# Weight sums in DRAM paced by ScalarE, in 4096 byte packets and for one product more, and the order of reads, heads and rows around them

## The chip, the cores and the metric

The kernel runs on one core of a Trainium2 chip. The metric is the device time of one execution in microseconds (us); the median of several runs is compared. A core has TensorE (PE, with PEld for its weight loads), VectorE (DVE), ScalarE (ACT), GpSimd (POOL) and SyncE (SP). Here SP issues most loads from DRAM, and POOL issues stores and all DMAs that add to what is already there (accumulate). Every engine, and each of these two issue queues, works through its instructions in the order in which the program wrote them, and waits on semaphores.

## What is computed

Two layers over 512 positions of width 2048. In each layer one projection of x feeds three groups of heads, every head's output is gated, one output projection follows, then a residual and a layer norm:

```python
h = jnp.einsum('bsd,dn->bsn', x, w_in)
(fq, fk, fv, fg, f_logit, dq, dk, dv, dg, iq, ik, iw, mq, mg) = jnp.split(h, offsets, axis=-1)
y_fox = fox_attention(heads(fq, 6), heads(fk, 6), heads(fv, 6), cum_logf) * silu(fg)
y_dsa = dsa_attention(rope(heads(dq, 6)), rope(heads(dk, 6)), heads(dv, 6), q_idx, k_idx, w_idx) * silu(dg)
y_mem = memory_attention(heads(mq, 4), k_mem, v_mem) * silu(mg)
y = jnp.einsum('bsn,nd->bsd', jnp.concatenate([y_fox, y_dsa, y_mem], -1), w_out)
x = layer_norm(ALPHA * x + y, ln_gain, ln_bias)
```

`fox_attention` (6 "f" heads) is causal attention with a bias per position; `dsa_attention` (6 "d" heads) attends to the 128 keys that an indexer picks for each query; `memory_attention` (4 "m" heads) attends to 256 memory tokens. All in float32; the kernel writes each float32 operand as a high and a low float32r part and takes three matmuls per product.

## The kernel before

**Stages of a layer.** Memory keys and values ("kv"); the indexer's projection ("index"); the value stage ("values"), which projects most columns; the head stage ("heads"), in which the last projections and the attention of the heads are interleaved; the output projection ("out"); and the layer norm, which makes the next layer's x.

**Chunks and halves.** All weights lie in DRAM as chunks of [128, 2048] (1 MB), in the order of use. A chunk is loaded in two halves of [128, 1024] into a pool of seven `raw` buffers (`load_w`, line 351), two chunks ahead where a buffer is free. `split_w` (line 433) turns a half into `whi` on ScalarE and `wlo` = raw - whi on VectorE, three halves ahead of the matmuls that use it. A chunk of a value or output product takes 24 matmuls of 128x512, 12 for each half.

**Seven products instead of eight.** The value and output projections use a Strassen-like scheme (`PRODUCTS`, line 82): P1, P7, Q4, P2, Q6, Q5, Q3, each with a left operand (A11, S3, A22, A12, S2, S1, S4) and a right operand that is a block of the weights or a sum of blocks (T1 to T4). The seven run over pairs of column blocks (six pairs for the values, two for the output). In the value stage P1, P7, P2, Q6, Q4 run, pair by pair; in the head stage Q5 and Q3. A product's two row blocks (`st` = 0, 1) accumulate in two PSUM banks. P2 goes on in the banks of P1, Q6 and Q4 in those of P7; Q3 goes on in the banks of Q5 right behind it.

**How the sums of weights are made.**
- "sum": in DRAM, by two DMAs on POOL's queue for a key of 1 MB: a copy of the first block (`sums[key]` made in `weight_sums`, line 565), later an accumulate of the second (`add_weights`, line 562). Before, these are T1 of all six value pairs, T3 of the first value pair, T3 of both output pairs: 18 keys a layer.
- "pair": T3 of the other value pairs. The second block is loaded into `other` slots, and VectorE adds it (`pair_w`, line 398).
- "grown": Q6's and Q4's weights grow out of those of P7, by VectorE in the value stage (`make_w`), by accumulating DMAs on POOL in the output stage (`grow_w`).
- "both": T1 of the output, S1's weights in Q5: quarters are loaded into slots by SP (`load_both`, 12 halves ahead) and the second block is added to them by accumulating DMAs on POOL (`add_both`, 8 halves ahead).

**What sets the order.** `all_sums` is a generator that issues one sum DMA and then lets some ticks pass (`paced`); in the value stage a chunk is one tick and a sum comes every two ticks, in "kv" and "heads" none. Outside the value stage `pool_waits` (line 551) goes ahead of each sum: VectorE writes a one-column `mark`, and a POOL instruction reads it into `seen`, so that POOL comes to the DMA no earlier than VectorE comes to the mark. In the value stage there is no mark. `val_out` (line 1255) reads both finished banks of a product when its last chunk is over. In the head stage a planner with a model clock (`flow`, `advance`) puts steps of the heads between the matmuls of the chunks: among the steps that fit, the one of the flow with the lowest age. At most `ACTIVE` heads are under way, and each start also needs `enough` slots, of 69 in all. `out_operands` prepares the output's left operands as such a flow. `top_keys` picks the indexer's keys on VectorE during the value stage; `residual_rows` (line 1480), in layer 1, loads 12 tiles of the layer's input on SP, multiplies and adds gain and bias on VectorE, and stores them on POOL, one tile per three ticks.

```python
        paced: yield {"out": 3, "index": 1 + n % 2}.get(now[1], steps)     # steps = PACE = 2
        enough: return live() + n <= (OUT_LIVE if now[1] == "out" else SLOTS - KT - 11)     # 44, or 42
        fits: return f[0] <= max(t, clock.at[eng]) and clock.at[eng] <= t + (SOON if now[1] == "heads" else LATER)
```

Of the kernel before, what the change touches and what calls it, by code (L numbers as in the profile page):

```python
# [20 lines left out]
DM = 2048  # L21
# [16 lines left out]
SLOTS = 69  # L38
# [20 lines left out]
BOTH_LOAD, BOTH_ADD = 12, 8  # L59
EARLY_AT = {0: 1, 1: 1, 2: 1, 3: 1, 4: 2, 5: 2}  # L60
ACTIVE = 2
OUT_LIVE = 44
# [44 lines left out]
PAIRED = {"T1": ((0, 0), (0, 1)), "T3": ((0, 1), (1, 1))}  # L107
# [26 lines left out]
def stream():  # L134
# [5 lines left out]
    def product(kind, l, name, pair, gs=(0, 1)):  # L140
        right = PRODUCTS[name][2]
        for g in gs:
            at = lambda step: where[kind, l, 2 * pair + step[1], 2 * step[0] + g]
            if name in GROWN:
                of, step = GROWN[name]
                src = ("grown", (of, at(step)))
            elif kind == "val" and right == "T3" and pair >= IN_DRAM:
                src = ("pair", tuple(at(step) for step in PAIRED[right]))
            elif kind == "out" and right == "T1":
                src = ("both", tuple(at(step) for step in PAIRED[right]))  # L150
            elif isinstance(right, str):
                src = ("sum", (kind, l, right, pair, g))
            else:
                src = ("wall", at(right))
# [103 lines left out]
def kernel(  # L258
# [42 lines left out]
    def enough(n):  # L301
        return live() + n <= (OUT_LIVE if now[1] == "out" else SLOTS - KT - 11)
# [48 lines left out]
    def load_w(i, pieces=2, some=(0, 1)):  # L351
        if i < len(chunks) and chunks[i][4][0] not in ("grown", "both"):
# [25 lines left out]

    def load_both(n):

        i, h = divmod(n, 2)
        if i < len(chunks) and chunks[i][4][0] == "both":
            src = half(wall[chunks[i][4][1][0]], h)
            t = raw.setdefault(i, [None, None])
            t[h] = [slot("both") for _ in range(2)]
            for c in range(2):
                nc.sync.dma_start(t[h][c], src[:, c * 512:(c + 1) * 512])

    def add_both(n):

        i, h = divmod(n, 2)
        if i < len(chunks) and chunks[i][4][0] == "both":
            src = half(wall[chunks[i][4][1][1]], h)
            for c in range(2):
                nc.gpsimd.dma_start(raw[i][h][c], src[:, c * 512:(c + 1) * 512], accum_op=ALU.add)

# [154 lines left out]
    def pool_waits():  # L551

        mark, seen = small("mark", 1), small("seen", 1)
        nc.vector.tensor_copy(mark, mhalf)
# [7 lines left out]
    def add_weights(key, src):  # L562
        nc.gpsimd.dma_start(sums[key], src, accum_op=ALU.add, max_dma_last_dim=4 * DM)

    def weight_sums(kind, l, names, pairs, some=(0, 1)):

        for name in names:
            for n in some:
                step = SUM_STEPS[name][n]
                for pair in pairs:  # L570
                    for g in range(2):
                        key = (kind, l, name, pair, g)
                        src = block(kind, l, pair, g, step)
                        if now[1] != "values":
                            pool_waits()
                        if n:
                            add_weights(key, src)
                        else:
                            sums[key] = dram.tile([P, DM], F32, name=uid("sum"))
                            nc.gpsimd.dma_start(sums[key], src)  # L580
# [19 lines left out]
    def all_sums():  # L600


        for l in range(DEPTH):
            yield from paced(value_sums(l))
            yield from paced(weight_sums("out", l, ("T3",), range(2)))
# [649 lines left out]
    def val_out(name, pair, ps):  # L1255


        if pair == PAIRS - 1:
            val_done.append(name)
            for k in [k for k in vleft if k[0] == PRODUCTS[name][1]]:  # L1260
                del vleft[k]
        j = 2 * pair
        for st in range(2):
            m1, m7 = ("M1", pair, st), ("M7", pair, st)
            if name == "P2" and j in VALUES:
                d = slot("vraw")
                nc.scalar.activation(d, ps[st], AF.Copy)
                begin(store_v(d, (j, st)), 1)
            elif name in ("P1", "P7"):
                d = vraw[m1 if name == "P1" else m7] = slot("vraw")  # L1270
                nc.scalar.activation(d, ps[st], AF.Copy)
            elif name == "P2":
                begin(store_turned(halves(ps[st]), (j, st)), 1)
            elif name == "Q6":
                d, e = slot("vraw"), vraw.pop(m7)
                nc.vector.scalar_tensor_tensor(d, ps[st], -1.0, vraw[m1], op0=ALU.mult,
                                               op1=ALU.subtract)
                nc.vector.tensor_tensor(e, e, d, op=ALU.add)
                begin(store_v(d, (j + 1, 2 + st)), 1)
                begin(store_v(e, (j + 1, st)), 1)  # L1280
            elif name == "Q4":
                d = vraw.pop(m1)
                nc.vector.tensor_tensor(d, d, ps[st], op=ALU.add)
                begin((store_v if j in VALUES else store_sum)(d, (j, 2 + st)), 1)
            elif j + 1 in VALUES:
                d = slot("vraw")
                nc.scalar.activation(d, ps[st], AF.Copy)
                begin(store_v(d, (j + 1, st + 2 * (name == "Q5")), True), 1)
            else:
                d = vraw.pop(("base", st))  # L1290
                nc.vector.tensor_tensor(d, d, ps[st], op=ALU.add)
                begin(store_sum(d, (j + 1, st + 2 * (name == "Q5"))))

    def load_base(name, pair):

        for st in range(2):
            r = st + 2 * (name == "Q5")
            assert stored[2 * pair + 1, r] == 1
            t = vraw["base", st] = slot("vraw")
# [277 lines left out]
    for i, (kind, l, j, col, _) in enumerate(chunks):  # L1577
# [17 lines left out]
        elif kind == "vs":  # L1595
# [3 lines left out]
            if col == 0:  # L1599
                if opens:  # L1600
                    chains[VAL_CHAIN[name], pair] = [bank("v"), bank("v")]
                if name in ("Q5", "Q3") and 2 * pair + 1 not in VALUES:
                    load_base(name, pair)
# [6 lines left out]
        for h in range(2):  # L1610
            n = 2 * i + h
            grow_w(n + 2)
            add_both(n + BOTH_ADD)
            load_both(n + BOTH_LOAD)
# [50 lines left out]
            elif kind == "vs":  # L1665
                for st in range(2):
                    for e in range(2):
# [3 lines left out]
                        advance()  # L1671
            elif kind == "mv":
# [40 lines left out]
        elif kind == "vs":  # L1713
            if col == 1:
                val_out(name, pair, zs)
# [43 lines left out]
        if kind == "vs" and (name, pair, col) == ("Q6", 0, 1) and l > 0:  # L1759
            begin(residual_rows(l), whole=True)  # L1760
        if kind == "vs" and (name, pair, col) == ("Q4", PAIRS - 1, 1):
            start_heads(l)
        if kind == "vs" and (name, pair, col) == ("Q5", PAIRS - 1, 0):
            flow(out_operands())
# [102 lines left out]
```

## Time and profile before

| | us |
|---|---|
| median of three runs | 1975.38 |
| lowest and highest | 1970.56, 1983.48 |
| the profiled execution, its own time | 1974.53 |
| its span, first to last instruction | 1972.8 |

The granted TensorE clock of the profiled execution is 0.983 on average. Nearly every instruction has line 242, that of the helper that records it, so the profile is read by the names of tiles: `v` are the banks of the value products, `c` those of other projections, `z` the output's, `vxh`/`vxl` and `xh`/`xl` the left operands' parts, `yh`/`yl` those of the output, `vraw` what is read from the banks. A row of a group reads: line, engine, operation, out<-in, shapes, xcount | busy us, mean ns | idle time of the engine just before these instructions, and what ended it. A row of the timeline: start, duration, engine, line, operation, tiles, and in brackets the idle time before. Of the DMA queues, q1 is SP's and q0 is POOL's.

The stages by the trace: layer 0's values about 148 to 569 us, heads to 791, output and norm to 985; layer 1's values 1129 to 1549, heads to 1771, output to 1962. Instructions that issue DMAs and those that wait are not counted as busy.

### The profile page before, as it was taken

To read this page: it belongs to the slowest core of one execution; us is meant where nothing else is said; L and a number is where in the kernel's file an instruction comes from. 1 tells how busy PE (TensorE), PEld (TensorE's weight loads), DVE (VectorE), ACT (ScalarE), POOL (GpSimd) and SP (SyncE) were. 2 spreads that over 40 slices of the span, in tenths; PEclk is the share of its full clock that TensorE was granted. 3 is DMA by queue.
4 is the path that set the end of the run, shared out by engine and by line. 5 is a ranking of instruction groups with operands and counts; after the bars stand their busy time and mean duration, and the time that the engine had idled before them with its cause. 6 is when DMAs were issued, how large, how long until landed. Compare 5 with 4: busy or idle time off the path is not lost.

```text
span 1972.8 us, 26387 instructions
## 1 busy us (share of the span) xinstructions
PE 1876.5 (95%) x8930; PEld 1576.4 (80%) x8930; DVE 1612.7 (82%) x2581; ACT 1081.5 (55%) x1702; POOL 384.4 (19%) x561
## 2 busy tenths in 40 slices
PE   9999799899999999999999998999999989999997
PEld 8998688687888787776899987877788878878865
DVE  6889588688788888787896897898887888888778
ACT  5775244344357777564576753343354577776443
POOL 0121011010133111252021111111110332112522
PEclk9999899899999999999999999999999999999999
DMA  9876878885589899999687878988955898999996
GB/s 350 302 218 203 275 239 248 260 240 199 171 224 255 256 238 247 206 258 242 203 296 251 221 213 271 302 264 283 285 202 150 240 258 241 249 226 239 275 250 149
DMA packets 233508, 478.38 MB, mean 242 GB/s; under 512 B 94289, under 2 KB 110673, under 8 KB 227933
## 3 DMA queue, kind: packets, MB, share of 16 engines
q1 hardware_dynamic: 190716, 306.78, 49.9%
q0 software_dynamic: 42080, 168.87, 33.5%
q8 instruction: 70, 1.15, 0.2%
q10 hardware_dynamic: 576, 1.05, 0.1%
q14 instruction: 66, 0.53, 0.1%
HBM read 400.05 MB, written 135.29 MB: 271 GB/s over the span
## 4 chain that ended last, share of the span: by engine, by line
PE 54%; DMA 19%; DVE 15%; ACT 5%; issue 5%; SPq 0%; POOL 0%; DVEq 0%; ACTq 0%; POOLq 0%
PE v L242 25%; PE c L242 16%; DMA other<-in_wall_dram 8%; PE z L242 7%; DVE wlo L242 6%; DMA both<-in_wall_dram 4%; DMA raw<-in_wall_dram 3%; PE po L242 2%; DVE raw L242 2%; ACT whi L242 2%; DVE acc L242 1%; PE ix L242 1%; DMA grown<-in_wall_dram 1%; PE s L242 1%; DVE z L242 1%
## 5 line engine op out<-in xcount | busy, mean ns | idle before, releaser
L242 ACT ACTIVATE whi<-raw 128x1024 fp32r<-128x1024 f32 (+1 forms) x481 | 502.4, 1055 | 527.6 <-PE v L242 238.1
L242 DVE TENSOR_TENSOR wlo<-raw,whi 128x1024 fp32r<-128x1024 f32 (+1 forms) x481 | 581.2, 1217 | 105.0 <-ACT whi L242 103.9
L242 PE MATMUL v<-wlo,vxh 128*128 128x512 f32 x768 | 304.2, 396 | 28.0 <-DVE wlo L242 27.7
L242 PE MATMUL v<-whi,vxh 128*128 128x512 f32 x768 | 305.9, 398 | 18.1 <-DVE vraw L242 13.0
L242 PE MATMUL v<-whi,vxl 128*128 128x512 f32 x768 | 302.1, 393 | 0.0
L242 PE MATMUL v<-wlo,xh 128*128 128x512 f32 x576 | 226.3, 393 | 11.6 <-DVE wlo L242 11.6
L242 PE MATMUL v<-whi,xh 128*128 128x512 f32 x576 | 225.4, 391 | 4.7 <-ACT whi L242 4.7
L242 PE MATMUL v<-whi,xl 128*128 128x512 f32 x576 | 225.1, 391 | 0.0
L242 PE MATMUL c<-xh,whi 128*128 128x512 f32 (+1 forms) x544 | 197.9, 364 | 0.0
L242 PE MATMUL c<-xh,wlo 128*128 128x512 f32 (+1 forms) x544 | 197.8, 364 | 0.0
L242 PE MATMUL c<-xl,whi 128*128 128x512 f32 (+1 forms) x544 | 197.7, 363 | 0.0
L242 PEld LDWEIGHTS v<-wlo,vxh 128*128 128x128 f32 x768 | 145.9, 190 | 63.8 <-DVE wlo L242 35.9
L242 PEld LDWEIGHTS v<-whi,vxh 128*128 128x128 f32 x768 | 145.8, 190 | 51.6 <-issue 9.8
L242 PE MATMUL z<-whi,yh 128*128 128x512 f32 (+1 forms) x434 | 173.1, 399 | 9.0 <-ACT whi L242 5.7
L242 PE MATMUL z<-wlo,yh 128*128 128x512 f32 (+1 forms) x434 | 172.0, 396 | 5.6 <-DVE wlo L242 5.5
L242 PE MATMUL z<-whi,yl 128*128 128x512 f32 (+1 forms) x434 | 170.7, 393 | 2.7 <-DVE yl L242 2.7
L242 PEld LDWEIGHTS v<-whi,vxl 128*128 128x128 f32 x768 | 145.8, 190 | 30.7
L242 PEld LDWEIGHTS v<-wlo,xh 128*128 128x128 f32 x576 | 108.7, 189 | 38.1 <-DVE wlo L242 15.8
L242 PEld LDWEIGHTS v<-whi,xh 128*128 128x128 f32 x576 | 108.7, 189 | 28.1 <-ACT whi L242 5.3
L242 PEld LDWEIGHTS v<-whi,xl 128*128 128x128 f32 x576 | 108.7, 189 | 22.4
L242 POOL DMA_DIRECT2D v<-vraw x72 | 45.2, 655 | 369.4 <-DVE vraw L242 282.7
L242 DVE TENSOR_TENSOR raw<-raw,other 128x512 f32<-128x512 f32 x80 | 53.2, 688 | 75.7 <-DMA other<-in_wall_dram 75.6
(206 smaller groups left out, 3518.1 us busy)
## 6 DMA issues: line engine op xcount, KB each, us to landing
raw<-in_wall_dram SPq DMA_DIRECT2D x331, 512.0 KB, 6.6
sum<-in_wall_dram POOLq DMA_DIRECT2D x36, 1024.0 KB, 12.2
raw<-sum SPq DMA_DIRECT2D x56, 512.0 KB, 7.1
other<-in_wall_dram SPq DMA_DIRECT2D x80, 256.0 KB, 13.2
v<-vraw POOLq DMA_DIRECT2D x72, 256.0 KB, 5.9
vt<-halves POOLq DMA_DIRECT2D x72, 256.0 KB, 6.5
grown<-in_wall_dram POOLq DMA_DIRECT2D x64, 256.0 KB, 8.2
vraw<-v SPq DMA_DIRECT2D x56, 256.0 KB, 4.6
```

The lines of the kernel that those rows point to most:

```text
L242: return f(*args, **kw)
```

## The change

- T1 of the output (S1's weights) becomes a "sum" like the others: 22 keys a layer. `load_both` and `add_both` go; Q5's output weights are loaded by `load_w` into `raw`.
- The copies and accumulates of the sums get `max_dma_last_dim=2 * DM`, packets of 4096 bytes; accumulates had 4 * DM, the copies no limit.
- `pool_waits` also runs in the value stage, and writes the mark there with ScalarE.
- `val_out` reads each bank when its own matmuls are done, ahead of those of the second; `load_base` (the stored rows to which Q5 and Q3 add) is issued one chunk earlier, with tiles of its own per product.
- Three heads may be under way, with 48 live slots instead of 42.
- `out_operands` gets age 0.0, the lowest.
- `residual_rows` begins at Q6 of the third pair instead of the first.

```diff
-BOTH_LOAD, BOTH_ADD = 12, 8
-ACTIVE = 2
-OUT_LIVE = 44
+ACTIVE = 3
+HEADS_LIVE, OUT_LIVE = 48, 44
...
-PAIRED = {"T1": ((0, 0), (0, 1)), "T3": ((0, 1), (1, 1))}
+PAIRED = {"T3": ((0, 1), (1, 1))}
...
-            elif kind == "out" and right == "T1":
-                src = ("both", tuple(at(step) for step in PAIRED[right]))
...
-        return live() + n <= (OUT_LIVE if now[1] == "out" else SLOTS - KT - 11)
+        return live() + n <= (OUT_LIVE if now[1] == "out" else HEADS_LIVE)
...
-    def load_both(n):
...
-                nc.sync.dma_start(t[h][c], src[:, c * 512:(c + 1) * 512])
-
-    def add_both(n):
...
-                nc.gpsimd.dma_start(raw[i][h][c], src[:, c * 512:(c + 1) * 512], accum_op=ALU.add)
...
-        nc.vector.tensor_copy(mark, mhalf)
+        if now[1] == "values":
+            nc.scalar.activation(mark, mhalf, AF.Copy)
+        else:
+            nc.vector.tensor_copy(mark, mhalf)
         nc.gpsimd.tensor_tensor(seen, mark, mhalf, op=ALU.mult)
...
-        nc.gpsimd.dma_start(sums[key], src, accum_op=ALU.add, max_dma_last_dim=4 * DM)
+        nc.gpsimd.dma_start(sums[key], src, accum_op=ALU.add, max_dma_last_dim=2 * DM)
...
-                        if now[1] != "values":
-                            pool_waits()
+                        pool_waits()
                         if n:
                             add_weights(key, src)
                         else:
                             sums[key] = dram.tile([P, DM], F32, name=uid("sum"))
-                            nc.gpsimd.dma_start(sums[key], src)
+                            nc.gpsimd.dma_start(sums[key], src, max_dma_last_dim=2 * DM)
...
-            yield from paced(weight_sums("out", l, ("T3",), range(2)))
+            yield from paced(weight_sums("out", l, ("T3", "T1"), range(2)))
...
-    def val_out(name, pair, ps):
...
-        for st in range(2):
...
-                nc.scalar.activation(d, ps[st], AF.Copy)
...
+    def val_out(name, pair, st, ps):
...
+            nc.scalar.activation(d, ps, AF.Copy)
...
-            t = vraw["base", st] = slot("vraw")
+            t = vraw["base", name, pair, st] = slot("vraw")
...
-                if name in ("Q5", "Q3") and 2 * pair + 1 not in VALUES:
-                    load_base(name, pair)
+            elif ahead_of(i + 1) and 2 * chunks[i + 1][2][1] + 1 not in VALUES:
+                load_base(*chunks[i + 1][2])
...
-            add_both(n + BOTH_ADD)
-            load_both(n + BOTH_LOAD)
...
                         advance()
+                    if col == h == 1:
+                        val_out(name, pair, st, zs[st])
...
             if col == 1:
-                val_out(name, pair, zs)
+                val_end(name, pair)
...
-        if kind == "vs" and (name, pair, col) == ("Q6", 0, 1) and l > 0:
+        if kind == "vs" and (name, pair, col) == ("Q6", 2, 1) and l > 0:
             begin(residual_rows(l), whole=True)
...
-            flow(out_operands())
+            flow(out_operands(), 0.0)
```

`val_end` holds what `val_out` did once per product: it notes that the product is done and drops its left operand.

More of the change, by code (lines that the diff above doesn't have):

```diff
@@ L351, in load_w @@
     def load_w(i, pieces=2, some=(0, 1)):
-        if i < len(chunks) and chunks[i][4][0] not in ("grown", "both"):
+        if i < len(chunks) and chunks[i][4][0] != "grown":
             kind, key = chunks[i][4]
@@ L377 @@
     others = {}
-    def load_both(n):
[L381 to L386, printed above, removed]
-                nc.sync.dma_start(t[h][c], src[:, c * 512:(c + 1) * 512])
-    def add_both(n):
[L391 to L394, printed above, removed]
-                nc.gpsimd.dma_start(raw[i][h][c], src[:, c * 512:(c + 1) * 512], accum_op=ALU.add)
     def pair_w(n):
@@ L1253, in val_left, with val_end @@
         return tuple(a[:, c:c + P] for a in vleft[name, i])
-    def val_out(name, pair, ps):
+    def val_end(name, pair):
         if pair == PAIRS - 1:
@@ L1261, in val_out @@
                 del vleft[k]
+    def val_out(name, pair, st, ps):
         j = 2 * pair
-        for st in range(2):
-            m1, m7 = ("M1", pair, st), ("M7", pair, st)
-            if name == "P2" and j in VALUES:
-                d = slot("vraw")
-                nc.scalar.activation(d, ps[st], AF.Copy)
[L1268 to L1292, printed above, removed]
@@ new lines, in val_out @@
+        m1, m7 = ("M1", pair, st), ("M7", pair, st)
+        if name == "P2" and j in VALUES:
+            d = slot("vraw")
+            nc.scalar.activation(d, ps, AF.Copy)
+            begin(store_v(d, (j, st)), 1)
+        elif name in ("P1", "P7"):
+            d = vraw[m1 if name == "P1" else m7] = slot("vraw")
+            nc.scalar.activation(d, ps, AF.Copy)
+        elif name == "P2":
+            begin(store_turned(halves(ps), (j, st)), 1)
+        elif name == "Q6":
+            d, e = slot("vraw"), vraw.pop(m7)
+            nc.vector.scalar_tensor_tensor(d, ps, -1.0, vraw[m1], op0=ALU.mult,
+                                           op1=ALU.subtract)
+            nc.vector.tensor_tensor(e, e, d, op=ALU.add)
+            begin(store_v(d, (j + 1, 2 + st)), 1)
+            begin(store_v(e, (j + 1, st)), 1)
+        elif name == "Q4":
+            d = vraw.pop(m1)
+            nc.vector.tensor_tensor(d, d, ps, op=ALU.add)
+            begin((store_v if j in VALUES else store_sum)(d, (j, 2 + st)), 1)
+        elif j + 1 in VALUES:
+            d = slot("vraw")
+            nc.scalar.activation(d, ps, AF.Copy)
+            begin(store_v(d, (j + 1, st + 2 * (name == "Q5")), True), 1)
+        else:
+            d = vraw.pop(("base", name, pair, st))
+            nc.vector.tensor_tensor(d, d, ps, op=ALU.add)
+            begin(store_sum(d, (j + 1, st + 2 * (name == "Q5"))))
```

## The prediction

> **What bounds the kernel now.** I read the page first, then the busy time by stage, then each stage's instruction groups, and last the timeline and the DMA queues around its longest waits.
>
> ```profile
> span 1972.8 us, 26387 instructions
> ...
> PE 1876.5 (95%) x8930; PEld 1576.4 (80%) x8930; DVE 1612.7 (82%) x2581; ACT 1081.5 (55%) x1702; POOL 384.4 (19%) x561
> ...
> PE 54%; DMA 19%; DVE 15%; ACT 5%; issue 5%; SPq 0%; POOL 0%; DVEq 0%; ACTq 0%; POOLq 0%
> PE v L242 25%; PE c L242 16%; DMA other<-in_wall_dram 8%; PE z L242 7%; DVE wlo L242 6%; DMA both<-in_wall_dram 4%; DMA raw<-in_wall_dram 3%; PE po L242 2%; DVE raw L242 2%; ACT whi L242 2%; DVE acc L242 1%; PE ix L242 1%; DMA grown<-in_wall_dram 1%; PE s L242 1%; DVE z L242 1%
> ```
>
> TensorE is busy for 95%. The chain names DMA for 19%, above all "other" (the second half of a paired weight) and "both" (S1's output weights), but a DMA on the chain costs only what TensorE stood still for. So I cut the span where the stages meet: values, heads and output of layer 0, then of layer 1.
>
> ```profile
> 148.00:569.00 421.00, 399.03 (x1740) 328.37 (x1739) 339.54 (x470) 180.97 (x202) 56.75 (x85) 0.97 0.75 230
> 569.00:791.00 222.00, 212.28 (x1070) 178.96 (x1069) 186.03 (x339) 160.97 (x315) 52.97 (x75) 0.99 0.90 244
> 791.00:985.00 194.00, 184.38 (x808) 149.22 (x807) 152.82 (x266) 100.65 (x167) 51.42 (x66) 0.96 0.89 229
> 1129.00:1549.00 420.00, 400.03 (x1730) 323.84 (x1729) 352.68 (x492) 178.20 (x201) 62.71 (x96) 0.99 0.80 249
> 1549.00:1771.00 222.00, 211.30 (x1072) 178.33 (x1071) 187.76 (x340) 162.13 (x315) 52.44 (x76) 1.00 0.91 243
> 1771.00:1962.00 191.00, 179.63 (x809) 144.80 (x807) 154.23 (x276) 96.56 (x167) 64.57 (x83) 0.97 0.93 234
> sum 1670.00, PE 1586.65 PEld 1303.52 DVE 1373.07 ACT 879.48 POOL 340.86; mean PE 264.44 PEld 217.25 DVE 228.84 ACT 146.58 POOL 56.81
> ```
>
> Columns: window, length, busy time of PE, PEld, DVE, ACT, POOL, granted clock, DMA share, GB/s. Length less PE is TensorE's idle time: 22.0, 9.7, 9.6 us in layer 0 and 20.0, 10.7, 11.4 in layer 1, together 1670.00 - 1586.65 = 83 us. Idleness also costs clock: 0.97 over 421 us of values is up to 12.6 us more. So all that this change can reach is about 110 us, and the two value stages hold half of it.
>
> **Sums: pace, packets, and S1's weights.** Weight sums are DRAM to DRAM DMAs on POOL's queue. In the value stage nothing holds them but POOL's own order: POOL stands before a store that waits for data, and when that is through it issues every sum written behind it at once. What that does, around the longest wait:
>
> ```profile
> 215.76 1.41 POOL L242 DMA_DIRECT2D sum<-in_wall_dram  x2
> 223.38 1.34 POOL L242 DMA_DIRECT2D sum<-in_wall_dram  x2 [6.21 <-DMA sum<-in_wall_dram]
> ...
> 237.49 0.69 DVE L242 TENSOR_TENSOR raw<-raw,other 128x512 f32<-128x512 f32 x1 [11.27 <-DMA other<-in_wall_dram]
> ...
> 241.37 0.80 PE L242 MATMUL v<-wlo,vxh 128*128 128x512 f32 x1 [10.53 <-DVE wlo L242]
> ```
>
> Four sums in 9 us; then VectorE waits 11.27 us for "other", and TensorE 10.53 us for the split behind it. The queues inside this stretch:
>
> ```profile
> q0 software_dynamic: 141, 1.02, 81.9%
> q1 hardware_dynamic: 182, 0.44, 20.4%
> ...
> q1 hardware_dynamic: 579, 2.11, 31.2%
> ...
> q0 software_dynamic: 139, 0.51, 107.6%
> ```
>
> In order: q0 (POOL) and q1 (SP) in 227 to 233 us, beside such sums (packets, MB, share of 16 engines); q1 alone in 240 to 260; q0 alone in 546.5 to 549, where POOL accumulates in 4096 byte packets. An 8192 byte accumulate packet holds an engine for 0.819 x 16 x 6 / (1.02 MB / 8192) = 0.63 us, a 4096 byte one for 1.076 x 16 x 2.5 / (0.51 MB / 4096) = 0.35 us, a load packet alone for 0.312 x 16 x 20 / (2.11 MB / 4096) = 0.19 us. Packet counts of the two queues are close, so they take turns. Loads then move 0.44 MB in 6 us = 73 GB/s beside an accumulate, while the quiet stretch needs 2.11 MB in 20 us = 105 GB/s. With 4096 byte packets, turn by turn: 16 x 4096 B / (0.35 + 0.19 us) = 121 GB/s, above what is needed. The price per MB is 256 x 0.35 / 16 = 5.6 us of all engines instead of 128 x 0.63 / 16 = 5.0.
>
> In the value stage each sum now waits for a ScalarE mark, which POOL's `seen` reads. That makes POOL issue a sum where the program has it, one per two chunks (2 x 24 matmuls), instead of two to four together. Queued behind the wait on POOL are only stores written later. The mark itself waits for POOL when three marks are unread; one per two chunks, that takes a lag of six chunks.
>
> ```profile
> L242 ACT ACTIVATION_READ_ACCUMULATOR bt<-bt,nm 128x1 f32 x48 | 9.2, 191 | 0.0
> ...
> L242 POOL TENSOR_TENSOR seen<-mark,mhalf x22: 180/392/1971, 69.9 to 1118.6; 128x1 f32<-128x1 f32 x22
> ...
> sum<-in_wall_dram POOLq DMA_DIRECT2D x36, 1024.0 KB, 12.2
> ...
> 455.00:515.00 60.00, 59.34 (x263) 48.78 (x261) 46.66 (x56) 24.76 (x26) 5.75 (x9) 1.00 0.55 198
> ```
>
> By the smallest ScalarE form above (191 ns), some 33 marks a layer are 6 us on an engine busy 181 of 421: nothing, as long as ScalarE stays half idle. The `seen` take 33 x 0.39 us (median) = 13 us a layer on POOL, which is busy 57 of 421: nothing either, unless they hold VectorE. The Trainium skill says that they can: page "SBUF — State Buffer", section "Who interferes with whom": a VectorE instruction with two SBUF inputs contends with a GpSimd instruction that reads SBUF, and the one that comes second blocks. The spread of `seen` from 180 to 1971 ns for one element looks like that, with POOL as the loser; with VectorE as the loser it is rival 4.
>
> There are 36 accumulates now, 18 a layer; S1's four keys a layer make it 22, and as many first copies. They come last, into the stretch where no sums run now (455 to 515 us: DMA 0.55, TensorE idle 0.66 us). 4 x 5.6 + 4 x half of that (a copy does not read its target) = 34 us of DMA more per value stage.
>
> Bounds for the value stages: from -42 of idle and up to -17 of clock (0.03 x 421 + 0.01 x 420; every wait gone) to +12 (the waits stay; 42 us over 36 accumulates is 1.2 us each, 1.5 with clock, and 8 more cost the same). I take 22 -> 5 and 20 -> 10, since layer 1's waits are short and VectorE has 353 of 420 us of work there: -27, with clock -33, and +7 for the new sums.
>
> **S1's weights in the output stage.** "both" is loaded in quarters on SP, added to on POOL, and only then split.
>
> ```profile
> both<-in_wall_dram POOLq DMA_DIRECT2D x16, 256.0 KB, 18.2
> ...
> L242 ACT ACTIVATE whi<-both 128x512 fp32r<-128x512 f32 x16 | 10.0, 631 | 22.1 <-DMA both<-in_wall_dram 21.0 <-PE z L242 1.1
> ...
> L242 PE MATMUL z<-wlo,yh 128*128 128x512 f32 x77 | 31.3, 406 | 1.3 <-DVE wlo L242 1.3
> L242 PE MATMUL z<-whi,yh 128*128 128x512 f32 x76 | 30.7, 404 | 2.7 <-ACT whi L242 2.7
> ...
> L242 PE MATMUL z<-wlo,yh 128*128 128x512 f32 x31 | 13.4, 433 | 1.9 <-DVE wlo L242 1.9
> ...
> L242 PE MATMUL z<-whi,yh 128*128 128x512 f32 x30 | 12.8, 426 | 3.0 <-ACT whi L242 3.0
> raw<-sum SPq DMA_DIRECT2D x56, 512.0 KB, 7.1
> ```
>
> (Landing in 855 to 935; ACT and PE in 880 to 940; PE in 1875 to 1905; raw<-sum on the page.) TensorE idles 4.0 and 4.9 us here; with the stage clocks of 0.96 and 0.97 against 1.00 it is about 7 each. Now these are plain loads, two chunks ahead, landing in 7.1 us; ScalarE reads them in one piece. -14 (between -16 and -4). POOL and 32 + 32 DMAs of this stage go as well.
>
> **Banks one by one.** TensorE's next product starts on the bank that is read first:
>
> ```profile
> L242 PE MATMUL v<-whi,vxh 128*128 128x512 f32 x192 | 77.8, 405 | 8.5 <-DVE vraw L242 6.3 <-ACT vraw L242 2.2
> ...
> L242 PE MATMUL v<-whi,vxh 128*128 128x512 f32 x192 | 77.0, 401 | 9.6 <-DVE vraw L242 6.7 <-ACT vraw L242 2.9
> ...
> L242 PE MATMUL v<-wlo,vxh 128*128 128x512 f32 x192 | 75.7, 394 | 1.2 <-DVE wlo L242 1.2
> ...
> 513.57 54.40 PE v L242 x240
> ...
> 676.58 1.28 DVE L242 TENSOR_TENSOR vraw<-vraw,v 128x512 f32<-128x512 f32 x2
> ...
> 677.32 0.50 PE L242 MATMUL v<-whi,vxh 128*128 128x512 f32 x1 [1.51 <-DVE vraw L242]
> ```
>
> 8.5 and 9.6 us per head stage, all at the step from Q5 to Q3, which share banks. The first read can be issued six matmuls earlier, ahead of what the planner puts in between, so at most 6 x 54.40 / 240 (a run of matmuls without a wait) = 1.4 us comes back at each of 12 steps. I take a bit over half of 18.1: -10 (0 to -16). The base rows one chunk earlier on SP hold two more slots and cost nothing while slots are free.
>
> **Output operands first.**
>
> ```profile
> 794.61 0.61 ACT L242 ACTIVATE yh<-y 128x512 fp32r<-128x512 f32 x1
> ...
> 795.27 0.50 PE L242 MATMUL z<-whi,yh 128*128 128x512 f32 x1 [1.67 <-ACT yh L242]
> ...
> 797.34 0.79 PE L242 MATMUL z<-whi,yl 128*128 128x512 f32 x1 [1.33 <-DVE yl L242]
> ```
>
> The output stage opens with 3.0 us of waiting for operands that stood last in the planner's order by age; age 0.0 puts them first: -6 in both layers (0 to -7).
>
> **Three heads, 48 slots, later rows.** TensorE has hardly another wait in the heads (1.2 us for wlo), so a third head brings it nothing directly; it moves VectorE work forward, where VectorE is busy 186 of 222 us. No row shows three heads; between -1 (that wait gone) and +36 a layer (VectorE's 36 free us all spent while TensorE waits). I take +3 in all, near the lower end, as the planner keeps VectorE within 1.5 us of TensorE.
>
> ```profile
> L242 DVE TENSOR_TENSOR z<-z,row x24: 678/687/694, 1184.7 to 1392.6; 128x512 f32<-128x512 f32 x24
> ```
>
> The residual rows (24 x 0.69 us of VectorE, 12 loads on SP, 12 stores on POOL) start two pairs later, so they end about 130 us later, near 1523, still inside the stage: 0 (-3 to +3).
>
> **Sum.** -33 + 7 - 14 - 10 - 6 + 3 = -53 us. The profiled execution took 1974.53 us, 1.7 beyond its span and 0.9 below the median of 1975.38; 1974.5 - 53 gives 1922 us.
>
> **Rivals.** (1) The waits only move: total DMA in the value stages rises from 0.75 and 0.80 of the engines by 34 of 421 us = 0.08, and "other" still lands late. For it: two loads of a pair need 1 MB at once. Against it: 455 to 515. Values then stay and pay +12; the rest gives -30 + 3: -15, 1960 us. (2) The marks pass early, since ScalarE runs ahead of TensorE, and sums still come in groups, in smaller packets only: the value stages give about 5 back, pay 7: -25, 1950 us. (3) The third head fills VectorE: the splits of the weights stand behind head work, and TensorE waits for them. Slower than before from the point where the two head stages lose over 56 us (the sum without its +3), 28 each, of VectorE's 36 free; at 36 each, 1991 us. Against it: TensorE idles only 1.2 us for wlo there now. (4) `seen` holds VectorE: 13 us a layer, 26 in both, come off the gain: -27, 1948 us. Against it: a wait needs VectorE on the chain, and in layer 0 it has 421 - 340 = 81 us free.
>
> **Chances.** The forecast 0.66 (its own range 1895 to 1947), rival 1 0.15, rival 2 0.07, rival 3 0.07, rival 4 0.05. The range takes in rivals 1, 2 and 4 and leaves out rival 3 and the forecast's ends: 1895 to 1966. About 1% (20 us) is what a measurement can tell here from no change: faster 0.66 + 0.07 + 0.05 = 0.78, same 0.15, slower 0.07.
>
> **What would show it.** Sums in the value stages stand singly, some 11 us apart, q0 without 64 KB or 8 KB accumulate packets; idle in the value stages under 20 us together; no "both"; waits from Q5 to Q3 under half; output opens without a wait for yh. Wrong would be: TensorE idle for "other" as before (rival 1), sums in groups (rival 2), more idle for wlo in the heads (rival 3), splits of the weights that grow longer beside `seen` (rival 4).

## The result, and the profile after

| | before | after |
|---|---|---|
| median, us | 1974.88 | 1925.20 |
| lowest and highest, us (4 runs each) | 1970.56 to 1983.48 | 1919.7 to 1934.0 |
| profiled execution, us | 1974.53 | 1924.92 |
| its span, us, and granted clock | 1972.8, 0.983 | 1923.2, 0.991 |

The ratio of after to before is 0.9747, with a 95% interval of 0.9698 to 0.9797: 50 us less, where 53 were predicted (1925 us against 1922). The page of the changed kernel:

```profile
span 1923.2 us, 26333 instructions
...
PE 1858.3 (97%) x8930; PEld 1571.9 (82%) x8930; DVE 1609.6 (84%) x2565; ACT 1087.8 (57%) x1752; POOL 416.5 (22%) x611
...
PE 61%; DVE 14%; DMA 12%; issue 7%; ACT 4%; SPq 1%; POOL 1%; DVEq 0%; POOLq 0%; ACTq 0%
...
sum<-in_wall_dram POOLq DMA_DIRECT2D x88, 1024.0 KB, 10.5
raw<-sum SPq DMA_DIRECT2D x72, 512.0 KB, 7.6
```

DMA has 12% of the chain of waits instead of 19%, and "both" is gone from it. The windows of the stages, cut at the same events as in the prediction:

```profile
148.00:550.00 402.00, 396.51 (x1744) 325.66 (x1743) 340.63 (x472) 185.85 (x238) 83.41 (x130) 1.00 0.87 263
550.00:773.00 223.00, 217.81 (x1109) 184.06 (x1108) 191.59 (x357) 170.26 (x336) 58.65 (x76) 0.99 0.88 246
773.00:947.00 174.00, 161.09 (x722) 133.32 (x721) 138.21 (x221) 86.20 (x135) 35.55 (x46) 0.96 0.83 215
1100.00:1514.00 414.00, 399.61 (x1740) 325.47 (x1739) 353.41 (x492) 183.42 (x236) 87.52 (x139) 1.00 0.89 272
1514.00:1737.00 223.00, 217.81 (x1115) 184.26 (x1115) 193.16 (x361) 172.10 (x337) 60.13 (x80) 1.00 0.90 252
1737.00:1912.00 175.00, 165.79 (x760) 137.79 (x759) 147.21 (x248) 85.40 (x138) 49.30 (x65) 0.98 0.87 223
sum 1611.00, PE 1558.62 PEld 1290.57 DVE 1364.22 ACT 883.24 POOL 374.57; mean PE 259.77 PEld 215.09 DVE 227.37 ACT 147.21 POOL 62.43
```

Length less PE gives the idle time: 5.5, 5.2, 12.9 us in layer 0 and 14.4, 5.2, 9.2 in layer 1, together 52 instead of 83. Both value stages run at full clock. Layer 0's has lost three quarters of its waits; layer 1's keeps 14.4 us of 20.0, where 10 were predicted. The output stages are no less idle than before (22.1 us against 21.0). They have a new wait, shown by PE's and ScalarE's timelines around it and by the DMA issues of that stretch:

```profile
825.61 1.62 PE L239 MATMUL pt<-ident,pr 128*128 128x128 f32 x6 [11.74 <-ACT pr L239]
```
```profile
805.76 1.14 ACT L239 ACTIVATE whi<-grown 128x512 fp32r<-128x512 f32 x2
821.12 0.63 ACT L239 ACTIVATE whi<-grown 128x512 fp32r<-128x512 f32 x1 [14.22 <-DMA grown<-sum]
...
824.16 1.90 ACT L239 ACTIVATE pr<-pr,rec 128x512 f32<-128x512 f32 x4
```
```profile
grown<-sum SPq DMA_DIRECT2D x8, 256.0 KB, 17.9
...
vraw<-vt SPq DMA_TRANSPOSE x1, 20.6
```

TensorE stands for `pr`, a tile of the last heads' attention. ScalarE would have it ready, but works in order and stands 14.22 us for a quarter of P7's output weights. These are issued late on SP and take 17.9 us to land. The transpose that SP issues just ahead of them takes 20.6 us in the same stretch; whether it slows them was not tried. In layer 1 the same wait is 7.05 us. No step of the prediction has it.

The sums of the value stage on POOL's timeline, 170 to 240 us:

```profile
176.12 0.58 POOL L239 DMA_DIRECT2D sum<-in_wall_dram  x1
187.29 0.88 POOL L239 DMA_DIRECT2D sum<-in_wall_dram  x1
198.47 0.95 POOL L239 DMA_DIRECT2D sum<-in_wall_dram  x1
206.06 0.60 POOL L239 DMA_DIRECT2D sum<-in_wall_dram  x1
222.48 0.57 POOL L239 DMA_DIRECT2D sum<-in_wall_dram  x1
235.69 0.93 POOL L239 DMA_DIRECT2D sum<-in_wall_dram  x1
```

They stand singly, 8 to 16 us apart, where before four came in 9 us. In layer 0, VectorE's waits for "other" fall from 45.7 us (the longest 11.3) to 25.5 (5.0), and TensorE's for the splits behind them from 22.0 to 5.4. In layer 1 they hardly change: 29.9 us before and 34.3 after for "other", 15.0 and 14.3 for the splits.

### The profile page after: what moved, and what is told of

It reads as the page before. It is cut to its first block, busy times and chain, and to the rows that moved or that the text cites. A ratio compares the mean times of both kernels' runs of the same rounds, so it can differ in the third digit from the quotient of the medians.

```text
span 1923.2 us, 26333 instructions
## 1 busy us (share of the span) xinstructions
PE 1858.3 (97%) x8930; PEld 1571.9 (82%) x8930; DVE 1609.6 (84%) x2565; ACT 1087.8 (57%) x1752; POOL 416.5 (22%) x611
## 3 DMA queue, kind: packets, MB, share of 16 engines
q0 software_dynamic: 55072, 177.26, 35.7%
## 4 chain that ended last, share of the span: by engine, by line
PE 61%; DVE 14%; DMA 12%; issue 7%; ACT 4%; SPq 1%; POOL 1%; DVEq 0%; POOLq 0%; ACTq 0%
PE v L239 26%; PE c L239 16%; PE z L239 13%; DMA other<-in_wall_dram 8%; DVE wlo L239 5%; PE po L239 2%; DVE raw L239 2%; DMA grown<-sum 2%; DVE acc L239 2%; PE ix L239 1%; PE s L239 1%; ACT bt L239 1%; DMA v<-vraw 1%; DMA raw<-in_wall_dram 1%; PE pt L239 1%
## 5 line engine op out<-in xcount | busy, mean ns | idle before, releaser
L239 ACT ACTIVATE whi<-raw 128x1024 fp32r<-128x1024 f32 (+1 forms) x497 | 521.1, 1055 | 482.8 <-PE v L239 206.3
L239 DVE TENSOR_TENSOR wlo<-raw,whi 128x1024 fp32r<-128x1024 f32 (+1 forms) x497 | 600.4, 1216 | 100.7 <-ACT whi L239 99.3
L239 PE MATMUL v<-wlo,vxh 128*128 128x512 f32 x768 | 302.4, 394 | 14.8 <-DVE wlo L239 14.5
L239 POOL TENSOR_TENSOR seen<-mark,mhalf 128x1 f32<-128x1 f32 x88 | 45.3, 515 | 635.3 <-ACT mark L239 442.9
L239 PEld LDWEIGHTS c<-xl,whi 128*128 128x128 f32 x544 | 102.1, 188 | 12.2
```

The source lines that it names most:

```text
L239: return f(*args, **kw)
```

## The experiments

Each kernel was run beside the kernel before on the same chip, and the ratio is to those runs. To compare the stages, both layers together, the table cuts each layer at its first value matmul, the first of Q5, and the first and last of the output. An entry is length, idle time of TensorE, both in us, worked out from the windows of one profiled execution. The kernels ran on several chips, so two of them are compared by their ratios as well as by their medians.

| kernel | median us, ratio to before | values | heads | output |
|---|---|---|---|---|
| before | 1974.9 | 901, 41.9 | 394, 20.4 | 380, 21.0 |
| after | 1925.2, 0.9747 [0.9698, 0.9797] | 872, 19.9 | 391, 10.4 | 361, 22.1 |
| no_marks | 1939.7, 0.9834 [0.9796, 0.9871] | 890, 31.0 | 391, 10.4 | 360, 20.4 |
| big_packets | 1929.9, 0.9771 [0.9729, 0.9812] | 872, 18.1 | 389, 10.4 | 356, 16.7 |
| before_paced | 1944.7, 0.9857 [0.9819, 0.9894] | 877, 20.8 | 394, 20.2 | 375, 21.1 |
| both_back | 1942.6, 0.9851 [0.9815, 0.9887] | 862, 12.0 | 390, 10.4 | 385, 31.0 |
| banks_back | 1959.3, 0.9913 [0.9886, 0.9940] | 872, 19.9 | 434, 30.6 | 360, 25.5 |
| rows_early | 1928.3, 0.9766 [0.9735, 0.9798] | 872, 19.9 | 390, 10.4 | 358, 17.8 |
| old_age | 1918.3, 0.9729 [0.9691, 0.9767] | 869, 17.7 | 390, 10.4 | 354, 15.8 |
| two_heads | 1909.4, 0.9682 [0.9651, 0.9713] | 865, 14.8 | 387, 12.5 | 356, 7.6 |
| two_48 | 1942.1, 0.9837 [0.9801, 0.9873] | 866, 14.7 | 386, 11.4 | 392, 39.9 |
| two_banks | 1923.8, 0.9778 [0.9734, 0.9821] | 872, 19.9 | 394, 20.1 | 361, 13.0 |
| early_p7 | 1912.4, 0.9715 [0.9686, 0.9743] | 869, 15.7 | 390, 10.4 | 355, 14.9 |
| two_spread | 1902.4, 0.9673 [0.9644, 0.9702] | 866, 17.0 | 385, 13.2 | 357, 11.0 |

The value stages of after and two_heads have the same edits and differ by 5 us of idle time (19.9 and 14.8), so differences of that size there are not read.

### Pace or packets

**no_marks** undoes the pace alone:

```diff
-                        pool_waits()
+                        if now[1] != "values":
+                            pool_waits()
```

> The changed kernel (1925 us) without the ScalarE marks in the value stages; packets of 4096 bytes and the sums of S1's weights stay. Theory (pace): POOL issues two to four sums together again, loads wait behind them, TensorE's idle time in the two value stages (5.5 and 14.4 us in the changed kernel) goes back to 15 to 20 each: about 1943 us. Rival (packets alone): with 4096 byte packets the loads get their 121 GB/s however many sums are queued, so the stages stay within 3 us of the changed kernel: 1925 to 1928 us.

Measured: 1939.7 us, 14 more than after. Nearly all of it is in layer 0, whose value stage is 445 us long instead of 430 (layer 1: 445 and 442). The same two pairs of sums as before come back on POOL's timeline, and behind them VectorE waits for "other" and TensorE for the split (rows of POOL, DVE and PE):

```profile
215.78 1.54 POOL L239 DMA_DIRECT2D sum<-in_wall_dram  x2
224.09 1.46 POOL L239 DMA_DIRECT2D sum<-in_wall_dram  x2 [6.77 <-DMA sum<-in_wall_dram]
```
```profile
231.01 0.69 DVE L239 TENSOR_TENSOR raw<-raw,other 128x512 f32<-128x512 f32 x1 [6.32 <-DMA other<-in_wall_dram]
```
```profile
236.41 0.79 PE L239 MATMUL v<-wlo,vxh 128*128 128x512 f32 x1 [5.54 <-DVE wlo L239]
```

It is the wait that the prediction showed at 241 us, 10.53 us there. With small packets it is half as long, but it does not go. Packets alone are not enough.

**big_packets** undoes the packets alone:

```diff
-accum_op=ALU.add, max_dma_last_dim=2 * DM)
+accum_op=ALU.add, max_dma_last_dim=4 * DM)
...
-nc.gpsimd.dma_start(sums[key], src, max_dma_last_dim=2 * DM)
+nc.gpsimd.dma_start(sums[key], src)
```

> The changed kernel with accumulates in 8192 byte packets and copies without a limit, as before; the marks stay. Theory (pace): a single sum holds the loads back for 5 us in 11, which two chunks of lead mostly cover: value stages 2 to 4 us more idle time each, about 1931 us. Rival (packets): loads fall to 73 GB/s beside every sum, and the 22 and 9.7 us of idle time of the kernel before come back for the most part: 1945 us or more.

Measured: 1929.9 us, not to be told from after. The value stages have the same length, 872 us. Once sums come singly, their packet size makes no difference that these runs can tell; that it counts where several sums stand in the queue together rests on the one wait above. POOL's queue holds the engines for 35.0% of the span with the large packets and 35.7% with the small ones. The Trainium skill (page "Perfetto Trace Analysis", section "DMA Optimizations") says that batching small transfers into larger ones, 2 KB into 4 KB or 8 KB for example, can improve throughput dramatically. No run here has sums in packets of 2 KB; between 4096 and 8192 bytes these runs show no gain.

**before_paced** puts marks and small packets into the kernel before, and nothing else:

```diff
+        if now[1] == "values":
+            nc.scalar.activation(mark, mhalf, AF.Copy)
...
-                        if now[1] != "values":
-                            pool_waits()
+                        pool_waits()
...
```

> The kernel before (1975 us) with the marks of ScalarE in the value stages and packets of 4096 bytes, and nothing else of the change. Theory, by the prediction's term: -33 us, all in the value stages, whose idle time falls from 22.0 and 9.7 us to 5 and 5 to 10, with the clock: about 1942 us. Rival: the value stages need the reads bank by bank or the later rows as well: -10 us or less, 1965.

Measured: -29 us (ratio 0.9857, so 21 to 36 us), 24 of it in the value stages: 19 in layer 0 and 5 in layer 1. They need nothing else of the change.

### S1's output weights

**both_back** takes T1 of the output out of the sums again and brings `load_both` and `add_both` back:

```diff
-            yield from paced(weight_sums("out", l, ("T3", "T1"), range(2)))
+            yield from paced(weight_sums("out", l, ("T3",), range(2)))
...
+            add_both(n + BOTH_ADD)
+            load_both(n + BOTH_LOAD)
```

> The changed kernel, but S1's output weights are loaded in quarters and added to in SBUF as before, and the eight sums a layer for them are gone. Theory, by the prediction's terms: the output stages lose 14, the value stages win back 7: about 1932 us, with ScalarE's and VectorE's waits for these tiles in the chain again. Rival: since the output stages of the changed kernel are together no less idle than before (12.9 and 9.2 us against 9.6 and 11.4), the weights were hardly worth anything: within 3 us of 1925.

Measured: 1942.6 us, 17 more than after (21 by the ratios). The table has the two sides apart: the output stages are 24 us longer, the value stages 10 us shorter without the eight sums a layer. The rival falls: the output stages of after are as idle as those of before because the new wait stands where the gain would show. The output's matmuls in layer 0, both_back and then after:

```profile
L242 PE MATMUL z<-wlo,yh 128*128 128x512 f32 x224 | 89.3, 399 | 4.5 <-DVE wlo L242 4.4
L242 PE MATMUL z<-whi,yh 128*128 128x512 f32 x224 | 89.3, 398 | 2.9 <-ACT whi L242 2.9
L242 PE MATMUL z<-whi,yl 128*128 128x512 f32 x223 | 87.9, 394 | 1.2 <-DVE yl L242 1.1
```
```profile
L239 PE MATMUL z<-whi,yh 128*128 128x512 f32 x224 | 88.0, 393 | 0.0
L239 PE MATMUL z<-wlo,yh 128*128 128x512 f32 x224 | 87.5, 391 | 0.0
L239 PE MATMUL z<-whi,yl 128*128 128x512 f32 x223 | 87.3, 391 | 1.2 <-DVE yl L239 1.1
```

With "both" TensorE waits 7.4 us more in this layer for the splits, and the same matmuls take 3.7 us longer (266.5 against 262.8 us).

### Banks, heads, slots

**banks_back** reads both banks after the last matmul again:

```diff
-                    if col == h == 1:
-                        val_out(name, pair, st, zs[st])
...
             if col == 1:
+                for st in range(2):
+                    val_out(name, pair, st, zs[st])
                 val_end(name, pair)
```

> The changed kernel, but both banks of a value product are read when its last chunk is over, as before. By the prediction +10: about 1935 us, and TensorE's waits for vraw in the head stages go from 3.1 us each back to 8 or 9. Rival: most of the shorter waits come from the base rows that are loaded a chunk earlier, or from the third head; then the waits stay below 5 us and the time within 3 us of 1925.

Measured: 1959.3 us, 34 more (the profiled execution has a span of 1963.6 us, 40 more). All of it is in the head stages, 43 us longer with only 20 us more idle time. The groups of PE in layer 0's head stage, banks_back above and after below:

```profile
L239 PE MATMUL v<-whi,vxh 128*128 128x512 f32 x192 | 81.8, 426 | 13.9 <-DVE vraw L239 10.5 <-ACT vraw L239 3.4
```
```profile
L239 PE MATMUL v<-whi,vxh 128*128 128x512 f32 x192 | 78.4, 408 | 3.1 <-DVE vraw L239 2.4 <-ACT vraw L239 0.6
```

Idle 13.9 us, more than before's 8.5, and each matmul is slower: 426 ns against 408. The granted clock of the two head stages is 0.94, against 0.99 and 1.00 in after, which is most of the rest. The reads are late because VectorE has head work first: the last matmul before the wait starts at 654.70 us, and VectorE reads the two banks at 657.26, behind `rope`, `pthl`, a split of weights and `ql` (busy for all of 655 to 660 us). These are windows of 5 us around two of the waits in banks_back, and the waits:

```profile
658.08 0.77 PE L239 MATMUL v<-whi,vxh 128*128 128x512 f32 x1 [2.99 <-DVE vraw L239]
```
```profile
702.42 0.79 PE L239 MATMUL v<-whi,vxh 128*128 128x512 f32 x1 [5.06 <-DVE vraw L239]
```
```profile
650.00:655.00 5.00, 5.00 (x25) 4.03 (x23) 4.94 (x8) 2.53 (x3) 0.27 (x1) 1.00 1.01 237
655.00:660.00 5.00, 2.01 (x7) 1.66 (x7) 5.00 (x10) 3.12 (x5) 0.00 (x0) 0.73 0.96 322
660.00:665.00 5.00, 5.00 (x16) 3.95 (x16) 2.36 (x6) 1.71 (x3) 1.55 (x2) 0.59 0.84 303
665.00:670.00 5.00, 5.00 (x24) 4.12 (x23) 3.30 (x8) 5.00 (x12) 0.00 (x0) 1.00 0.43 110
...
705.00:710.00 5.00, 5.00 (x18) 4.26 (x18) 2.76 (x4) 2.49 (x4) 0.45 (x1) 0.65 0.62 210
710.00:715.00 5.00, 5.00 (x24) 4.14 (x23) 1.24 (x3) 3.27 (x6) 0.00 (x0) 1.00 0.00 0
```

After these waits of 3 and 5 us TensorE has a granted clock of 0.59 and 0.65 for some 5 us (the third number from the end of a window's row). At 0.59, 5 us do the work of 3, so a wait of 3 us that is followed by this costs about 5 (an estimate).

**two_banks** makes the same edit where two heads run, with 42 slots and the old age.

> Two heads, 42 slots and the old age (1909 us), and besides both banks of a value product are read when its last chunk is over. With three heads that cost 34 us, where the prediction had 10. Theory: the prediction's 10 holds for two heads, and the third head's work on VectorE makes the late reads later: 1919 to 1921 us, with 8 to 10 us of waits for vraw in each head stage. Rival: the reads bank by bank are worth 30 us whatever the heads do: 1940 us.

Measured: 1923.8 us against 1909.4 without the edit, 14 more (19 by the ratios), and the head stages are 7 us longer. The groups of PE in layer 0's head stage, two_banks and then two_heads:

```profile
L239 PE MATMUL v<-whi,vxh 128*128 128x512 f32 x192 | 77.9, 406 | 8.8 <-DVE vraw L239 5.7 <-ACT vraw L239 2.2 <-ACT qh L239 0.9
```
```profile
L239 PE MATMUL v<-whi,vxh 128*128 128x512 f32 x192 | 77.9, 406 | 4.1 <-DVE vraw L239 3.2 <-ACT vraw L239 0.8
```

The waits for `vraw` are 7.9 us against 4.0, and in layer 1 8.0 against 4.0. So with two heads the reads are worth about what the prediction had, and the third head makes a late read dearer.

**two_heads** undoes the third head, the slots and the new age together:

```diff
-ACTIVE = 3
-HEADS_LIVE, OUT_LIVE = 48, 44
+ACTIVE = 2
+HEADS_LIVE, OUT_LIVE = 42, 44
...
-            flow(out_operands(), 0.0)
+            flow(out_operands())
```

> The changed kernel with two heads and 42 slots again, and the output's operands at their old age. The prediction has +3 for the third head and -6 for the operands, so undone together: about +3, 1928 us. Theory: the new wait of the output stage (11.7 us in layer 0 and 7.2 in layer 1, TensorE for ScalarE's pr, behind P7's late weights) comes from these edits: it goes, the opening's waits come back (3 to 4 us a layer), about 1912 us. Rival: the wait comes from the output's weights and the earlier start of the stage; it stays, and the time is 1928 us or more.

Measured: 1909.4 us, 16 less than after (13 by the ratios, whose intervals just overlap). The output stages have 7.6 us of idle time instead of 22.1. The new wait is gone; ScalarE's waits for P7's weights in layer 0 are down to these (columns: in total, times, longest; two_heads):

```profile
ACT whi L239 <- DMA grown<-sum: 3.4, 3, 1.3
```

**old_age** undoes the age alone (the last line of that diff).

> The changed kernel with three heads and 48 slots, but the output's operands at their old age, last in the planner's order. By the prediction +6: about 1931 us, with the opening waits for yh and yl back (3 to 4 us a layer against 1.6). If the new wait for pr comes from head work that the operands push back into the output stage, it goes here, and the time is 1910 to 1915 us; if it comes from the third head alone, it stays.

Measured: 1918.3 us, 7 less than after, and the intervals overlap. The opening's wait comes back (3.98 us in layer 0 against 1.08; the trace names a load of weights, but it ends with VectorE's `yl`), and the wait for `pr` falls to 2.4 us in layer 0 and 3.4 in layer 1. The new age has exchanged the one for the other, and won nothing that shows.

**two_48** is two_heads with 48 slots, so the third head and the slots are told apart:

```diff
-HEADS_LIVE, OUT_LIVE = 42, 44
+HEADS_LIVE, OUT_LIVE = 48, 44
```

> Two heads and the old age, but 48 slots for the head stages: between the kernel with three heads, 48 slots and the old age (1918 us) and the one with two heads and 42 slots (1909 us). Theory: the difference of 9 us is the third head, so this is 1909 us within 3, with ScalarE's waits for P7's weights as short as with 42 slots. Rival: it is the slots, which heads take from the output's weights: 1918 us, with these waits at 8 us or more in layer 0.

Measured: 1942.1 us, 33 more than with 42 slots, and more than the rival had said. All of it is in the output stages (39.9 us idle). PE in layers 0 and 1, and ScalarE's waits in them:

```profile
830.53 1.83 PE L239 MATMUL pt<-ident,pr 128*128 128x128 f32 x7 [11.81 <-ACT pr L239]
```
```profile
1801.35 2.05 PE L239 MATMUL pt<-ident,pr 128*128 128x128 f32 x8 [21.23 <-ACT pr L239]
```
```profile
ACT whi L239 <- DMA grown<-sum: 23.1, 6, 13.8
```
```profile
ACT whi L239 <- DMA grown<-sum: 25.9, 4, 23.1
```

With two heads the six slots alone bring the wait, so it does not need the third head. P7's output weights are the exception among the loads of weights: they go into the same 69 slots that the heads use, not into `raw`. With up to 48 of them in use by heads, the loads of P7's weights stand on SP for slots that PE has yet to give back, and behind loads and transposes of the last heads (10.4 us for PE's `z` in two_48, 765 to 835 us, and none in two_heads, which stands 8.9 us for `po` there). The same two kinds of waits stand on SP in the changed kernel, 785 to 826 us:

```profile
SPq L358 <- PE z L239: 9.5, 6, 3.8
SPq L358 <- DMA vraw<-vt: 6.9, 1, 6.9
SPq L1336 <- PE s L239: 4.6, 1, 4.6
```

L358 loads P7's weights, L1336 is a transpose of a head. At 48 slots the third head even helps (old_age against two_48: 24 us). Three heads with 42 slots were not tried.

**early_p7** is the changed kernel with P7's weights loaded three chunks ahead:

```diff
-                if late_half:
+                for k in (i + 2, i + 3):
+                    p7 = k < len(chunks) and chunks[k][0] == "out" and chunks[k][2][0] == "P7"
+                    if p7 and len(raw.get(k, ())) == h:
+                        load_w(k, 2, (h,))
+                if i + 2 < len(chunks) and chunks[i + 2][0] == "out" and chunks[i + 2][2][0] == "P7":
+                    pass
+                elif late_half:
                     load_w(i + 2, 2, (h,))
```

> The changed kernel (three heads, new age), but P7's output weights are loaded three chunks ahead instead of two; nothing else moves on SP. Theory: TensorE's 11.7 and 7.2 us for pr are ScalarE standing for these weights; they fall below 3 us each, and the time to 1905 to 1910 us. Rival: the third head's steps are late by themselves, or SP then waits for slots: the waits stay, under this name or another, and the time is within 4 us of 1925.

Measured: 1912.4 us, 13 less than after (6 by the ratios, whose intervals overlap) and 2 above the range that was expected. The time alone does not decide; the waits do. ScalarE's waits for these weights in layer 0 fall from 21.1 us to 3.0 (775 to 835 us, after and then early_p7):

```profile
ACT whi L239 <- DMA grown<-sum: 21.1, 4, 14.2
```
```profile
ACT whi L239 <- DMA grown<-sum: 3.0, 2, 1.9
```

The wait for `pr` is gone in both layers; 3.5 us for the split of those weights stand for it in layer 0, and 5.4 us for splits in layer 1. So the wait for `pr` was the weights' late landing, not the heads' own pace. Between 800 and 815 us four quarters of these weights still take 18.3 us to land here: they are asked for earlier, not moved faster.

### Rows, and a better version

**rows_early** begins the residual rows at the first pair again (`("Q6", 0, 1)`).

> The changed kernel with the residual rows begun at the first pair again. By the prediction nothing: 1925 us within 3. The value stage of layer 1 has 14.4 us of idle time against 5.5 in layer 0, most of it between 1300 and 1480 us, where the rows now are. Theory: the rows cost what the stage has more, wherever they stand: the waits move ahead to 1180 to 1400 us and stay about 14 us. Rival: the later place saves, or costs, 5 us or more.

Measured: 1928.3 us, and 14.5 us of idle time in layer 1's value stage against 14.4. Their place costs and saves nothing. But the waits go with the rows, as the theory had it: between 1150 and 1300 us, where the rows now begin, TensorE idles 8.7 us instead of 0.4, and between 1300 and 1400 us 5.1 instead of 11.5. So the waits that layer 1's value stage has more than layer 0's follow the rows.

**two_spread** is two_heads with a pace that is to leave the double loads free:

```diff
+            if now[1] == "values":
+                yield 1 + (n % 3 == 0)
+                while any(c[4][0] == "pair" for c in chunks[at_chunk[0] + 2:at_chunk[0] + 4]):
+                    yield 1
...
```

> Two heads, 42 slots and the old age (1909 us), and in the value stages no sum is issued while the double loads of P7's pairs are due; the sums come 1.33 chunks apart in between. Theory: what is left of the waits in the value stages (15 us in layer 1, 5 in layer 0) is accumulates on top of those loads: half of it goes, about 1900 us. Rival: the DMA engines are busy for nine tenths of these stages anyway, and the waits move to the chunks between: 1909 us or slower.

Measured: 1902.4 us, ratio 0.9673 against two_heads' 0.9682: no difference that these runs can tell. Layer 0's values have 2.3 us of idle time instead of 4.0, layer 1's 14.7 instead of 10.8. The edit clears the double loads in part: in layer 1 one or two sums are still issued beside the first loads of each pair (at 1133.48 and 1136.61 us, with loads at 1133.94 and 1135.67), and then none for 34 to 40 us. Fewer sums on top of these loads did not shorten layer 1's waits. VectorE has 89 of 100 us of work there (1300 to 1400 us in two_spread):

```profile
1300.00:1400.00 100.00, 90.14 (x385) 71.68 (x386) 88.62 (x119) 42.18 (x54) 17.21 (x30) 1.00 0.82 253
```

The rows' work on VectorE would fit both that and rows_early; no run leaves the rows out, and they also load on SP and store on POOL. Both two_heads and two_spread beat the kernel before by 3.2 and 3.3%, and all their runs (1901.9 to 1912.8 us) lie below all of the changed kernel's.

## Why the prediction was right, point by point

The time came out 3 us off, and the stages close by, on the table's cut: values -26 predicted (-33 + 7) and -29 measured, heads -7 (-10 + 3) and -3, output -20 (-14 - 6) and -19. That agreement is in part luck. 54 matmuls of the output stages' windows before are no longer in them after, and the head stages' windows have 55 more: head work has moved across the cut. In the output stages new waits for `pr` of 18.8 us fill the idle time that was to go. The terms did less well than the stages.

- **Value stages, -33.** About right in size: before_paced gave -29 by itself, 24 of it in the value stages. Right in the cause for layer 0, the order on POOL. In layer 1 the waits for "other" and for the splits hardly changed, and 14.4 us of idle time stayed where 10 were taken. (The upper bound of +12 uses less clock than the lower one: 42 + 17 us over 36 sums is 1.6 us each, so +13.) The price of packets failed as well. That loads beside an accumulate of large packets get 73 GB/s and need 105 was read from a stretch in which four sums stood in the queue. For a single sum the two chunks of lead are enough with large packets too (big_packets).
- **New sums, +7.** 10 by both_back's value stages. Between both_back and after DMA there rises by 0.08 and 0.06 of the engines (0.79 to 0.87, 0.83 to 0.89), where 0.08 was worked out.
- **"both", -14.** Too small for the changed kernel: 24 us in the output stages. The 4.0 us of waits that the term took in layer 0 are those of the whole stage of the kernel before; in layer 1 its window of 30 us caught 4.9 of 7.2 us. In both_back layer 0 has 7.4 us of waits for splits and 3.7 us of slower matmuls. What the weights were worth in the kernel before alone was not measured.
- **Banks, -10.** About right for the kernel it was read from: 14 to 19 us with two heads, of which only 7 are in the head stages, and waits for `vraw` from 8.5 and 9.6 us to 3.1. With the third head it is 34: the late reads wait longer behind head work on VectorE, and the clock falls behind the longer waits. The term took the edits as independent.
- **Output operands, -6.** Wrong: no gain that shows. The opening's waits did go (from 3.0 us to 1.1 in layer 0), but head work that was pushed back waits later in the same stage (old_age).
- **Three heads and 48 slots, +3.** Wrong in size and place: with the age, undoing them gives 16 us. The bound was taken from VectorE. The prediction thought of slots for the base rows alone ("cost nothing while slots are free"), and gave the six slots more for the heads no price. With two heads they cost 33 us, by making P7's weights late (two_48).
- **Residual rows, 0.** Right.

So that -53 came out within 3 us is partly luck: "both" and the banks, which were too small, made up for the slots and the age. No step of the prediction had P7's weights.

**The rivals.** (1) The waits only move: no in layer 0, where TensorE waits 5.4 us for the splits instead of 22.0 though DMA is busier. In layer 1 it is half true: the waits for "other" are as long as before, but the sums are not shown to be their cause (rows_early, two_spread). (2) The marks pass early: no; the sums stand singly, and no_marks shows what (2) would have looked like, 1940 us against the 1950 of the prediction. (3) The third head fills VectorE: no; TensorE's wait for `wlo` in layer 0's head stage is 2.1 us, against 1.2 before. (4) `seen` holds VectorE: no. The splits on the pages, before and after:

```profile
L242 DVE TENSOR_TENSOR wlo<-raw,whi 128x1024 fp32r<-128x1024 f32 (+1 forms) x481 | 581.2, 1217 | 105.0 <-ACT whi L242 103.9
```
```profile
L239 DVE TENSOR_TENSOR wlo<-raw,whi 128x1024 fp32r<-128x1024 f32 (+1 forms) x497 | 600.4, 1216 | 100.7 <-ACT whi L239 99.3
...
L239 POOL TENSOR_TENSOR seen<-mark,mhalf 128x1 f32<-128x1 f32 x88 | 45.3, 515 | 635.3 <-ACT mark L239 442.9
```

With 88 `seen` instead of 22 the mean split takes 1216 ns, as before. By the rule of the Trainium skill (page "SBUF — State Buffer", section "Who interferes with whom") the one of the two engines that comes second is blocked. VectorE is not seen to be: the splits take no more time, and none waits for `seen`. Whether POOL is, these traces leave open: its `seen` take 183 to 1981 ns for one element, but no row says why.

## What to carry to other kernels

Issue background DMAs singly, each behind a mark of the engine whose pace they are to follow; then their packet size matters little (big_packets), while their number still costs: eight sums a layer were 10 us of value stages (both_back). When an edit hands out more of a shared pool of buffers, look for the load that allocates from it last, and for the in-order engine that will stand for that load with other work behind it. Price edits that touch the same engine together: what one saves depends on the other.

## What the runs showed of the hardware

A short wait can cost more than its length. In banks_back the clock was 0.59 and 0.65 in the windows behind waits of 2.99 and 5.06 us, and 20 us more of idle time made two stages 43 us longer. The length of the wait alone does not tell: behind a wait of 2.13 us the changed kernel had 0.66 (590 to 595 us), and behind one of 2.44 us the kernel before kept 1.00 (640 to 650 us). The Trainium skill (page "TensorE: Matmul & The Clock Gate", section "What's actually happening") has TensorE fall to half its clock after one idle window of about 3.4 us. The trace agrees for the wait of 5.06 us; the waits of 2.99 and 2.13 us are shorter than that window, and the clock fell all the same.
